# Output projection of a Hawk/HGRN2 step: low parts on VectorE, first touch of x2 on ScalarE with x1 added by DMA, the last head's small products over all four pairs

## The chip, the cores and the metric

The kernel runs on one core of one Trainium2 chip. The core has a matrix engine (TensorE, PE in the profile; its weight loads are listed apart as PEld), a vector engine (VectorE, DVE), a scalar engine (ScalarE, ACT), a general engine (GpSimd, POOL) and a sync engine (SyncE, SP) that here only issues DMA transfers. ScalarE and GpSimd can issue transfers too. Each engine works through its own list of instructions in order and waits on semaphores for the others. The metric is the device time of one execution in microseconds; the time of a kernel is the median of its runs.

## The reference

One inference step of a two-layer decoder trunk on 1024 prompt tokens and 8 x 4 sample tokens: 1056 token columns (TOK). Layer 0 is a recurrent block (RG-LRU), layer 1 a gated linear recurrence with 8 heads (HGRN2); then a final RMSNorm. What matters here is the end of layer 1:

```python
def _hgrn_layer(x, g_norm, w_in, lb, o_gain, w_out, S0):
    ...
    o = o * lax.rsqrt(jnp.mean(o * o, axis=-1, keepdims=True) + EPS) * o_gain.reshape(H_B, DV_B).astype(jnp.float32)
    y = (o.reshape(Bsz, T, INNER_B) * jax.nn.silu(gate)).astype(x.dtype)
    return x + y @ w_out, S_T.astype(x.dtype)
```

`x` at this point is called x1 in the kernel (the output of layer 0), and `x + y @ w_out` is x2. Both have 1024 features, that is 8 rows of 128 partitions by 1056 columns of float32.

## The kernel before, in words

**High and low parts.** A float32 product is made of three fast products (`mm3`, lines 243 to 245). Each operand is split into a high part, a copy rounded by ScalarE (`S.copy`), and a low part, the value minus its high part. `subtract` (line 330) writes the subtraction for either VectorE or GpSimd. `low` makes the low part in another way: ScalarE writes the negated high part and an accumulating DMA issued by GpSimd (line 317) adds the value.

**The planner.** `Flow` collects all operations of a layer with their engine, an estimated duration, and the keys that they read and write. `plan` runs them through a model of the engines and fixes each engine's order; the operations are then issued in that order. An operation with `both=True` on VectorE is taken to be lengthened while GpSimd is at work: in the model it ends only after GpSimd's current work, whatever that work is (`free["POOL"]`).

**Heads.** Layer 1 goes through heads 0 to 7. The recurrence of a head is cut into four bursts of small products, `burst1` to `burst4`. `burst1(h)` holds the first levels of head h and the transposed keys and values of head h - 1; `burst2(h)` two more levels and the states of head h - 1 (its last state updates are VectorE's L1257, which free a PSUM bank for the product of line 1250); `burst3(h)` the output products of head h - 1 and two levels of h; `burst4(h)` the gating of head h - 1, the last levels of h and a part of its values. `seven` makes the projections of a head with seven block products in place of eight (Strassen's scheme, Winograd's form); the digits of an order such as `"126b74b53"` are these seven block products, each `b` is a place where the next burst goes in.

**Output projection.** For heads 0 to 5 y is kept in DRAM in the sums that the scheme needs (`ysum`). `youts` loads 21 of them as tiles of 528 columns, into what becomes the low part; ScalarE makes the high part (line 1623) and the low part is a subtraction, seven of them on VectorE and fourteen on GpSimd (`YSUB`). `seven_out` then makes two of the eight rows of x2 at a time: four pairs, each in the order that `LAST` gives for it. For each pair it loads four blocks of w_out of 384 columns, GpSimd makes four combinations of them (line 1673, `combine`), and each of the seven blocks is split: the high part by ScalarE (line 1665), the low part by GpSimd, as `BYDVE` is empty. Each of the seven steps makes two products of 264 columns into one of four PSUM banks, and VectorE adds what is in the bank to x2 (line 1687, `add`): 14 additions a pair. Before that x2 was filled with x1 by a load on SP's queue, one per row. The bursts that are left of head 7 and its gating go in at the `b` of `LAST`: two in each of the first three pairs, none in the last. After the gating of heads 6 and 7, `splits` splits their y.

**The end.** What heads 6 and 7 add to x2 is made by ordinary products (lines from 1751; the addition is line 1831) in three column ranges, row by row, with the final norm behind them.

Of the kernel before, what the change touches and what calls it, by code (L numbers as in the profile page):

```python
# [24 lines left out]
NW, NXO, NRAW = 4, 3, 3  # L25
K1 = 6
NMM = 3
BYDVE = ()
HC = 1
FQ0, FQ, GV = "1267b4b35", "12b675b43", "126b74b53"  # L30
SPOTS, SPOTS0 = (6, 9, 0, 2), (2, 5, -1, -1)
LAST = "12b675b43", "126b74b53", "12b675b43", "1267543"
K2 = 8 - K1
RM, SM = 3, 6
OUT = ((0, 424), (424, 376), (800, 256))
# [16 lines left out]
class Flow:  # L52
# [49 lines left out]
    def plan(self, key, stop=None):  # L102

        n = len(self.ops)
        left = [len(o[3]) for o in self.ops]
        ready = [0.0] * n
        wait = {e: [] for e in self.ENGINES}
        free = dict.fromkeys(self.ENGINES, 0.0)
        dma = 0.0
        for i in range(n):  # L110
            if not left[i]:
                wait[self.ops[i][0]].append(i)
        starts, ends, took, order = [0.0] * n, [0.0] * n, [0.0] * n, []
        for _ in range(n):
            t0, e = min((max(free[e], min(ready[i] for i in q)), e) for e, q in wait.items() if q)
            q = wait[e]
            i = min((j for j in q if ready[j] <= t0), key=lambda j: (key[j], j))
            q.remove(i)
            order.append(i)
            _, us, _, _, _, kb, _, both = self.ops[i]  # L120
            if both and free["POOL"] > t0:
                us = max(us, free["POOL"] - t0 + us - 0.13)
            starts[i] = t0
            free[e] = end = t0 + us
            if kb:
                dma = max(dma, t0 + 2.6) + kb / 250.0
                end = dma - 2.15 - kb / 250.0
            ends[i] = max(free[e], dma if kb else 0.0)
            took[i] = us
            if i == stop:  # L130
                break
            for j in self.after[i]:
                ready[j] = max(ready[j], end + self.lag(i, j))
# [78 lines left out]
def tile_trunk(ctx: ExitStack, tc: tile.TileContext, xT, prm, hc, w0, wg, wo0, w1, wo1, s_in,  # L212
# [34 lines left out]
    def run(*gens):  # L247
        for g in gens:
            for _ in g:
                pass  # L250
# [47 lines left out]
    with ExitStack() as l0:  # L298
# [24 lines left out]
            fl.add("DVE", 0.13 + 0.0011 * n, emit, r, w, prio, both=both)  # L323

        def pool(n, emit, r, w, prio=5):
            fl.add("POOL", 0.1 + 0.00245 * n, emit, r, w, prio)

        def subtract(e, n, b, x, a, r, w, prio):

# [605 lines left out]
    with ExitStack() as l1:  # L935
# [49 lines left out]
        def eight(*name):  # L985
            return [(*name, i, x) for i in range(2) for x in range(4)]
# [367 lines left out]

        def burst1(h):
            s = next(side)
            run(together([*([levels01(h, *s)] if h < H else []), *([keys_(h - 1, *s), values(h - 1, (1,), *s)] if h else [])]))

        def burst2(h):
            s = next(side)  # L1360
# [5 lines left out]

        def burst4(h):
            s = next(hg)
            run(together([*([gated(h - 1, *s)] if h else []), *([levels3264(h, *s), values(h, (0,))] if h < H else [])]))
            if h:  # L1370
                summed_y(h - 1)

# [251 lines left out]
                subtract(YSUB[j], HT, lo, lo.bitcast(F32), hi, (hk, lk), (lk,), 2)  # L1624
                youtput[p].append((hi, lo, (hk, lk)))

        YSUB = V, G, G
        youtput = {p: [] for p in range(1, 8)}
        for p in map(int, GV.replace("b", "")):
            youts(p)  # L1630
# [1 line left out]
        def splits(k, cs, eng):  # L1632

            for c in cs:
# [6 lines left out]
        old = [GK, [("s", i) for i in range(6)], eight("A", 0), eight("A1"), eight("B"), eight("B2"), [("VT", i) for i in range(4)],  # L1641
               [("Gc", l) for l in (1, 2, 4, 8, 16, 32)]]

        def seven_out(m, order, at):

            nonlocal rawq
            bursts = iter(at)
            u = 384
# [36 lines left out]
            def add(i, a, z):  # L1685
                o, ok = x2[i][:, a:a + QT], ykeys(Y2 + i, a, QT)
                dve(QT, lambda: V.tensor_tensor(o, o, z[0], op=ALU.add), (z[1], *ok), ok, 0)

            for c in order:
                if not c.isdigit():  # L1690
                    next(bursts)()
                    continue
                p = int(c)
                if p == steps[-1]:
                    rawq = [(o, k) for o, k in freed]
                hi, lo, wk = parts[p]
                for x in range(2):
                    ps, pk = chains[p in (2, 3, 5)][x]
                    new = p in (1, 2, 5) or apart and p == 3
                    ops = [(a[:, x * QT:x * QT + QT], b[:, x * QT:x * QT + QT], k) for a, b, k in youtput[p]]  # L1700

                    def emit(ps=ps, ops=ops, hi=hi, lo=lo, new=new):
                        for j, (uh, ul, _) in enumerate(ops):
                            w = slice(128 * j, 128 * j + 128)
                            mm3(ps[:, :QT], (hi[:, w], lo[:, w]), uh, ul, new and j == 0, j == 2, True)

                    pe(1.09, emit, (*wk, *(k for o in ops for k in o[2])), (pk,))
                    z = ps[:, :QT], pk
                    first, second = x * QT, HT + x * QT
                    if p == 1:  # L1710
                        add(m, first, z)
                    elif p == 2:
                        add(m, first, z)
                    elif p == 6:
                        add(m, second, z)
                    elif p == 7:
                        add(m + 1, second, z)
                    elif p == 4:
                        add(m + 1, first, z)
                    else:  # L1720
                        if p == 5:
                            add(m + 1, second, z)
                        if p == 3 or apart:
                            add(m, second, z)
                n = steps.index(p) + NW
                if n < 7:
                    split(steps[n])

        def then(*fs):
            return lambda: [f() for f in fs]  # L1730

        ends_ = [lambda: burst3(H - 1), then(lambda: burst4(H - 1), lambda: splits(6, range(NCH), V)), lambda: burst1(H), lambda: burst2(H),
                 lambda: burst3(H), then(lambda: burst4(H), lambda: splits(7, range(NCH), V))]
        for i, order in enumerate(LAST):
            seven_out(2 * i, order, ends_[2 * i:2 * i + 2])
        side = cycle(banks8[NMM:4])
        raws = cycle([r for r in rawq if r[1][0] == "raw"])

# [181 lines left out]
```

## Time and profile before

| | us |
|---|---|
| median of 3 runs | 1079.52 (1077.19 to 1080.65) |
| the profiled execution | 1078.1 |
| its span, first to last instruction | 1076.3 |
| PE busy | 1045.6 (97%) |
| DVE busy | 788.9 (73%) |
| ACT busy | 667.1 (62%) |
| POOL busy | 543.9 (51%) |

A row of instructions names the line, the engine, the operation, and then output<-inputs by the program's tile names, with the count; a row of the timeline begins with its start and its duration in us, and in square brackets stand the idle time ahead of it and what ended that. A tile name is the name of the buffer: `xl` and `t` are operands of the output projection's `youts` as well as of the projections before it, `wlo` low parts of weights, `sg`, `ST`, `R`, `a` and `k` large buffers used for many things. The output projection's four pairs run from about 941 to 1035 us, the end from there to 1076.

### The profile page before, as it was taken

How to read it: one execution, taken by the hardware profiler on the slowest of the kernel's cores; microseconds unless marked ns; L12 is line 12 of the kernel's file. 1: busy time of each engine (PE TensorE's matmuls, PEld its weight loads, DVE VectorE, ACT ScalarE, POOL GpSimd, SP SyncE). 2: the span in 40 equal slices, each digit the busy share in tenths (PEclk: the TensorE clock that was granted, in tenths of full speed). 3: DMA queues.
4: the chain of work that ended last, by engine and by line, in shares of the span. 5: the costliest groups of instructions: out<-in, count | busy, mean ns of one | idle time of the engine just before them, and what ended most of it. 6: DMA issues, size and time to landing. Idle time of an engine off the chain costs nothing.

```text
span 1076.3 us, 25929 instructions
## 1 busy us (share of the span) xinstructions
PE 1045.6 (97%) x10092; PEld 1016.2 (94%) x10092; DVE 788.9 (73%) x1526; ACT 667.1 (62%) x1494; POOL 543.9 (51%) x566
## 2 busy tenths in 40 slices
PE   9999999999999999999979999999999999889996
PEld 9999999999999999999979999999899989889995
DVE  7999996887997787283987555666566766988546
ACT  6578657867665964243577676868485846663333
POOL 3425353353543546455444454544545454679565
PEclk9999999999999999999999999999999999989998
DMA  9211112124832786364684665657485632754114
GB/s 297 63 28 42 56 49 71 58 61 127 260 113 65 211 255 186 102 236 141 175 200 100 145 145 120 157 116 167 102 199 114 152 109 84 257 165 139 58 35 162
DMA packets 90331, 143.24 MB, mean 133 GB/s; under 512 B 11104, under 2 KB 55904, under 8 KB 90208
## 3 DMA queue, kind: packets, MB, share of 16 engines
q1 hardware_dynamic: 75808, 116.79, 34.3%
q0 software_dynamic: 12096, 22.03, 12.4%
q10 hardware_dynamic: 2304, 2.77, 0.8%
q8 instruction: 79, 1.29, 0.5%
q14 instruction: 44, 0.36, 0.1%
HBM read 81.60 MB, written 33.05 MB: 107 GB/s over the span
## 4 chain that ended last, share of the span: by engine, by line
PE 80%; DVE 13%; DMA 3%; issue 2%; ACT 1%; POOL 1%; POOLq 0%; ACTq 0%; SPq 0%; DVEq 0%
PE mm L243 22%; PE mm L244 22%; PE mm L245 22%; PE hg L1058 2%; PE hg L574 1%; DVE xl L330 1%; DVE R L1040 1%; DVE t L330 1%; PE hg L1275 1%; PE hg L1167 1%; PE hg L1221 1%; PE hg L243 1%; PE hg L244 1%; PE hg L245 1%; PE hg L1277 1%
## 5 line engine op out<-in xcount | busy, mean ns | idle before, releaser
L243 PE MATMUL mm<-xh,whi 128*128 128x352 f32 (+1 forms) x1147 | 355.2, 310 | 10.5 <-DVE sg L1537 4.1
L244 PE MATMUL mm<-xl,whi 128*128 128x352 f32 (+1 forms) x1147 | 349.3, 305 | 0.0
L245 PE MATMUL mm<-xh,wlo 128*128 128x352 f32 (+1 forms) x1147 | 349.1, 304 | 0.0
L243 PEld LDWEIGHTS mm<-xh,whi 128*128 128x128 f32 x1147 | 216.3, 189 | 11.8 <-DVE sg L1537 5.0
L244 PEld LDWEIGHTS mm<-xl,whi 128*128 128x128 f32 x1147 | 216.4, 189 | 4.1 <-issue 2.6
L245 PEld LDWEIGHTS mm<-xh,wlo 128*128 128x128 f32 x1147 | 216.3, 189 | 0.0
L330 POOL TENSOR_TENSOR wlo<-wraw,whi 128x512 fp32r<-128x512 f32 (+1 forms) x83 | 112.5, 1363 | 98.5 <-ACT whi L385 75.4
L243 PE MATMUL mm<-t,whi 128*128 128x264 f32 x408 | 119.3, 292 | 1.1 <-ACT k L1514 0.6
L245 PE MATMUL mm<-t,wlo 128*128 128x264 f32 x408 | 116.6, 286 | 2.1 <-DMA wlo<-wraw 2.1
L244 PE MATMUL mm<-t,whi 128*128 128x264 f32 x408 | 116.5, 286 | 0.0
L506 DVE SCALAR_TENSOR_TENSOR k<-xb,prm_sb,k 128x352 f32<-128x352 f32 (+2 forms) x144 | 90.2, 637 | 10.7 <-ACT k L503 6.0
L245 PEld LDWEIGHTS mm<-t,wlo 128*128 128x128 f32 x408 | 77.4, 190 | 2.5 <-DMA wlo<-wraw 2.5
L243 PEld LDWEIGHTS mm<-t,whi 128*128 128x128 f32 x408 | 77.7, 190 | 2.1 <-ACT k L1514 0.8
L244 PEld LDWEIGHTS mm<-t,whi 128*128 128x128 f32 x408 | 77.8, 191 | 0.1
L317 POOL DMA_DIRECT2D wlo<-wraw x51 | 44.6, 887 | 61.6 <-ACT wlo L316 35.4
L1537 DVE TENSOR_TENSOR k<-mm,k 128x264 f32<-128x264 f32 x72 | 30.5, 430 | 53.8 <-PE mm L245 50.5
L589 POOL TENSOR_TENSOR k<-X 128x352 f32<-128x352 f32 x36 | 44.9, 1256 | 47.7 <-DVE R L590 38.5
L243 PE MATMUL mm<-yh,whi 128*128 128x352 f32 x153 | 49.9, 326 | 0.0
L317 POOL DMA_DIRECT2D wlo<-R x30 | 28.5, 951 | 41.3 <-ACT wlo L316 34.9
L245 PE MATMUL mm<-yh,wlo 128*128 128x352 f32 x153 | 49.4, 323 | 0.0
L244 PE MATMUL mm<-yl,whi 128*128 128x352 f32 x153 | 49.4, 323 | 0.0
L385 ACT CAST whi<-wraw 128x512 fp32r<-128x512 f32 (+1 forms) x63 | 36.3, 591 | 20.1 <-DMA wraw<-in_w_dram 11.3
(413 smaller groups left out, 2722.4 us busy)
## 6 DMA issues: line engine op xcount, KB each, us to landing
wraw<-in_w_dram SPq DMA_DIRECT2D x88, 256.0 KB, 3.1
wlo<-wraw POOLq DMA_DIRECT2D x51, 256.0 KB, 4.1
wlo<-R POOLq DMA_DIRECT2D x30, 256.0 KB, 4.2
wraw<-in_wo_dram SPq DMA_DIRECT2D x37, 192.0 KB, 2.5
ysum<-sg SPq DMA_DIRECT2D x9, 528.0 KB, 4.4
si<-in_s_in_dram SPq DMA_DIRECT2D x8, 512.0 KB, 4.4
R<-in_w_dram SPq DMA_DIRECT2D x16, 256.0 KB, 3.8
out_ss_out_dram<-si SPq DMA_DIRECT2D x8, 512.0 KB, 2.7
```

The source lines that it names most:

```text
L243: T.matmul(out, wh, xh, start=first, stop=False, skip_group_check=chained)
L244: T.matmul(out, wh, xl, start=False, stop=False, skip_group_check=chained)
L245: T.matmul(out, wl, xh, start=False, stop=last, skip_group_check=chained)
L317: fl.add("POOL", 0.93, lambda: G.dma_start(dst.bitcast(F32), src, accum_op=ALU.add), (*r, *w), w, prio, n / 2)
L330: emit = lambda: e.tensor_tensor(b, x, a.bitcast(F32), op=ALU.subtract)
L385: act(m, lambda hi=hi, raw=raw, m=m: S.copy(hi[:, :m], raw[:, :m]), rk, (hk,), prio)
L506: dve(u, lambda src=src, dst=dst, sh=sh, k=k: V.scalar_tensor_tensor(dst, sh(src, k), pc("cw", 12 * k + m), dst, op0=ALU.mult, op1=ALU.add ...
L574: fl.add("PE", 0.62, lambda ps=ps, i=i, c=c: T.matmul(ps[:96, :CH], gs[:, i, :], ST[:96, chunk(c)], start=True, stop=True), (("gs",), *((" ...
L589: pool(CH, lambda x=x, a=a, b=b: G.tensor_tensor(x, a.bitcast(F32), b.bitcast(F32), op=ALU.add), (ak, bk), (xk,), 3)
L1040: dve(n // 2, lambda sv=sv, dv=dv, s=s, f=f: V.tensor_tensor(dv[:, :, s, :], sv[:, :, s, :], f, op=ALU.mult), (*sk, *gk), dk if i == o els ...
L1058: T.matmul(ps[32 * j:32 * j + 32, n * w:n * w + w], B[:, o:o + 32], q(slice(o, o + 32)), start=True, stop=True, tile_position=(0, 32 * j))
L1537: dve(QT, lambda: V.tensor_tensor(o[0], z[0], u[0], op=ALU.add), (z[1], u[1]), (o[1],), 0)
```

## The change

1. `YSUB` and `BYDVE`: all 21 low parts of the `youts` and all seven low parts of w_out's blocks in each pair are made by VectorE.
2. `put`: the first thing written to a part of x2 is a ScalarE copy from PSUM (steps 1, 6, 7 and 4 of each pair); the later ones stay VectorE additions. x1 is no longer loaded into x2 at the start of a pair: at its end, two accumulating DMAs issued by GpSimd add x1 to the finished rows.
3. `LAST` and `ends_`: the bursts are taken one after the other over all four pairs: pair 1 gets `burst3(7)` and the values' transposes of head 7, pair 2 `burst4(7)` with the split of head 6's y and `burst1(8)`, pair 3 `burst2(8)` and `burst3(8)`, pair 4 `burst4(8)` with the split of head 7's y. `values` leaves `burst4(7)` and `burst1(8)` for that.
4. The buffers of x2's rows are given out in another order, so that each is free by then.
5. The planner: only GpSimd's tensor operations that go through `pool` hold VectorE in the model, no longer its DMA issues and powers. This touches both layers.

```diff
-BYDVE = ()
+BYDVE, BYDMA = (1, 2, 3, 4, 5, 6, 7), ()
...
-LAST = "12b675b43", "126b74b53", "12b675b43", "1267543"
+LAST = "12b675b43", "12b67b453", "12b675b43", "1b267543"
...
-            if both and free["POOL"] > t0:
-                us = max(us, free["POOL"] - t0 + us - 0.13)
+            if both and e == "DVE" and held > t0:
+                us = max(us, held - t0 + us - 0.13)
             starts[i] = t0
             free[e] = end = t0 + us
+            if both and e == "POOL":
+                held = end
...
         def pool(n, emit, r, w, prio=5):
-            fl.add("POOL", 0.1 + 0.00245 * n, emit, r, w, prio)
+            fl.add("POOL", 0.1 + 0.00245 * n, emit, r, w, prio, both=True)
...
-            run(together([... *([keys_(h - 1, *s), values(h - 1, (1,), *s)] if h else [])]))
+            run(together([... *([keys_(h - 1, *s), values(h - 1, (1,) if h < H else (), *s)] if h else [])]))
...
-            run(together([... *([levels3264(h, *s), values(h, (0,))] if h < H else [])]))
+            run(together([... *([levels3264(h, *s)] if h < H else []), *([values(h, (0,))] if h < H - 1 else [])]))
...
-        YSUB = V, G, G
+        YSUB = V, V, V
...
-        x2 = [Gs, KR[:, :TOK], R[:, 2], R[:, 1], Bs, B2, VT, Gc]
+        x2 = [Gs, KR[:, :TOK], R[:, 2], VT, R[:, 1], Gc, Bs, B2]
...
-                dma(x2[i], x1d[i], (), ykeys(Y2 + i, 0, TOK), 3, 528)
...
-                subtract(V if p in BYDVE else G, u, lo, raw, hi, (rk, hk), (lk,), 2)
+                if p in BYDMA:
+                    low(u, lo, raw, (rk,), (lk,), 2)
+                else:
+                    subtract(V if p in BYDVE else G, u, lo, raw, hi, (rk, hk), (lk,), 2)
...
+            def put(i, a, z):
+                o, ok = x2[i][:, a:a + QT], ykeys(Y2 + i, a, QT)
+                act(QT, lambda: S.copy(o, z[0]), (z[1],), ok, 0)
...
                     if p == 1:
-                        add(m, first, z)
+                        put(m, first, z)
                     elif p == 2:
                         add(m, first, z)
                     elif p == 6:
-                        add(m, second, z)
+                        put(m, second, z)
                     elif p == 7:
-                        add(m + 1, second, z)
+                        put(m + 1, second, z)
                     elif p == 4:
-                        add(m + 1, first, z)
+                        put(m + 1, first, z)
...
+            for i in (m, m + 1):
+                ok = ykeys(Y2 + i, 0, TOK)
+                fl.add("POOL", 0.93, lambda i=i: G.dma_start(x2[i], x1d[i], accum_op=ALU.add), ok, ok, 3, 528)
...
-        ends_ = [lambda: burst3(H - 1), then(lambda: burst4(H - 1), lambda: splits(6, range(NCH), V)), lambda: burst1(H), lambda: burst2(H),
-                 lambda: burst3(H), then(lambda: burst4(H), lambda: splits(7, range(NCH), V))]
+        ends_ = iter([lambda: burst3(H - 1), lambda: run(values(H - 1, (0, 1))), then(lambda: burst4(H - 1), lambda: splits(6, range(NCH), V)), lambda: burst1(H), lambda: burst2(H),
+                      lambda: burst3(H), then(lambda: burst4(H), lambda: splits(7, range(NCH), V))])
```

More of the change, by code (lines that the diff above doesn't have):

```diff
@@ L108, in plan @@
         free = dict.fromkeys(self.ENGINES, 0.0)
-        dma = 0.0
+        dma = held = 0.0
         for i in range(n):
@@ L1356, in burst1 @@
             s = next(side)
-            run(together([*([levels01(h, *s)] if h < H else []), *([keys_(h - 1, *s), values(h - 1, (1,), *s)] if h else [])]))
+            run(together([*([levels01(h, *s)] if h < H else []), *([keys_(h - 1, *s), values(h - 1, (1,) if h < H else (), *s)] if h else [])]))
         def burst2(h):
@@ L1368, in burst4 @@
             s = next(hg)
-            run(together([*([gated(h - 1, *s)] if h else []), *([levels3264(h, *s), values(h, (0,))] if h < H else [])]))
+            run(together([*([gated(h - 1, *s)] if h else []), *([levels3264(h, *s)] if h < H else []), *([values(h, (0,))] if h < H - 1 else [])]))
             if h:
@@ L1638, in splits @@
                 subtract(eng, CH, b, x, a, (*xk, ("yh", k, c)), (("yl", k, c),), 1)
-        x2 = [Gs, KR[:, :TOK], R[:, 2], R[:, 1], Bs, B2, VT, Gc]
-        old = [GK, [("s", i) for i in range(6)], eight("A", 0), eight("A1"), eight("B"), eight("B2"), [("VT", i) for i in range(4)],
-               [("Gc", l) for l in (1, 2, 4, 8, 16, 32)]]
+        x2 = [Gs, KR[:, :TOK], R[:, 2], VT, R[:, 1], Gc, Bs, B2]
+        old = [GK, [("s", i) for i in range(6)], eight("A", 0), [("VT", i) for i in range(4)], eight("A1"),
+               [("Gc", l) for l in (1, 2, 4, 8, 16, 32)], eight("B"), eight("B2")]
         def seven_out(m, order, at):
             nonlocal rawq
-            bursts = iter(at)
-            u = 384
+            bursts, u = at, 384
             slot = {n: (t[:, :u], k) for n, (t, k) in zip(("11", "21", "22", "12", "s"), rawq)}
@@ L1727, in seven_out @@
                     split(steps[n])
+            for i in (m, m + 1):
+                ok = ykeys(Y2 + i, 0, TOK)
+                fl.add("POOL", 0.93, lambda i=i: G.dma_start(x2[i], x1d[i], accum_op=ALU.add), ok, ok, 3, 528)
         def then(*fs):
             return lambda: [f() for f in fs]
-        ends_ = [lambda: burst3(H - 1), then(lambda: burst4(H - 1), lambda: splits(6, range(NCH), V)), lambda: burst1(H), lambda: burst2(H),
-                 lambda: burst3(H), then(lambda: burst4(H), lambda: splits(7, range(NCH), V))]
+        ends_ = iter([lambda: burst3(H - 1), lambda: run(values(H - 1, (0, 1))), then(lambda: burst4(H - 1), lambda: splits(6, range(NCH), V)), lambda: burst1(H), lambda: burst2(H),
+                      lambda: burst3(H), then(lambda: burst4(H), lambda: splits(7, range(NCH), V))])
         for i, order in enumerate(LAST):
-            seven_out(2 * i, order, ends_[2 * i:2 * i + 2])
+            seven_out(2 * i, order, ends_)
         side = cycle(banks8[NMM:4])
```

## The prediction

> **What bounds the kernel now.** I read the page first: how much of the span TensorE (PE) works, and what the chain that ended last is made of.
>
> ```profile
> span 1076.3 us, 25929 instructions
> ...
> PE 80%; DVE 13%; DMA 3%; issue 2%; ACT 1%; POOL 1%; POOLq 0%; ACTq 0%; SPq 0%; DVEq 0%
> ```
>
> TensorE sets the time, but 13% of the chain is VectorE (DVE), so there is a stretch where it leads. The busy time by stretch (columns: length, then busy us and count for PE, PEld, DVE, ACT, POOL, then granted clock, DMA share, GB/s) shows where.
>
> ```profile
> 917.00:932.00 15.00, 15.00 (x183) 14.77 (x182) 14.77 (x25) 11.51 (x28) 7.43 (x6) 1.00 0.89 292
> 932.00:944.00 12.00, 7.23 (x186) 6.31 (x185) 11.73 (x10) 4.30 (x12) 9.00 (x7) 1.00 0.43 156
> 944.00:957.00 13.00, 11.98 (x100) 11.39 (x98) 12.79 (x22) 9.99 (x33) 11.41 (x10) 1.00 0.58 178
> 957.00:974.00 17.00, 13.97 (x247) 12.86 (x248) 14.43 (x29) 7.15 (x18) 14.42 (x12) 0.80 0.49 159
> ...
> 1000.00:1035.00 35.00, 35.00 (x286) 34.16 (x286) 17.41 (x43) 11.96 (x39) 23.22 (x26) 1.00 0.20 63
> ```
>
> From 917 to 957, VectorE is busy 39.3 of 40 us, and from 932 PE is not. This is the end of the last head's projections and the first pair of the output projection. From 1000 PE is full and VectorE half empty. PE's waits between 930 and 975 (us in total, times, longest):
>
> ```profile
> PE hg L1250 <- DVE si L1257: 3.0, 1, 3.0
> PE mm L243 <- ACT os L1245: 2.5, 1, 2.5
> PE mm L243 <- issue: 2.2, 1, 2.2
> ```
>
> That is 7.7 us. Two of the three lead back to VectorE: ScalarE's copy L1245 itself waited for VectorE's L1065, which stood behind three long instructions. Their rows, then POOL's of the same time:
>
> ```profile
> ACT os L1245 <- DVE attns L1065: 7.7, 1, 7.7
> ```
> ```profile
> 932.35 5.34 DVE L330 TENSOR_TENSOR xl<-xl,xh 128x528 fp32r<-128x528 f32 x1
> 937.62 2.51 DVE L1049 TENSOR_TENSOR sg<-sg 128x264 f32<-128x264 f32 x1
> 940.05 1.52 DVE L330 TENSOR_TENSOR t<-t,t 128x528 fp32r<-128x528 f32 x1
> ```
> ```profile
> 931.82 1.51 POOL L1199 TENSOR_TENSOR vb<-vst,bm 96x512 fp32r<-96x512 f32 x1
> 933.29 2.57 POOL L330 TENSOR_TENSOR xl<-xl,xh 128x528 fp32r<-128x528 f32 x2
> 935.83 1.29 POOL L330 TENSOR_TENSOR t<-t,t 128x528 fp32r<-128x528 f32 x1
> 937.10 1.45 POOL L330 TENSOR_TENSOR wlo<-wraw,whi 128x384 fp32r<-128x384 f32 x1
> ```
>
> With POOL idle, the same shapes take far less:
>
> ```profile
> 923.76 0.70 DVE L330 TENSOR_TENSOR xl<-xl,xh 128x528 fp32r<-128x528 f32 x1
> ...
> 942.51 0.68 DVE L1040 TENSOR_TENSOR sg<-sg 128x512 f32<-128x512 f32 x1
> ...
> 956.73 0.41 DVE L1687 TENSOR_TENSOR ST<-ST,mm 128x264 f32<-128x264 f32 x1
> ```
>
> So 9.37 us stand where 0.70 + 0.41 + 0.70 = 1.8 would do: 7.6 us held. The 5.34 us row ends at 937.69, about 0.6 after the POOL row of 935.83 ends: VectorE was passed over by four POOL instructions in a row. [...]
>
> The clock adds to it: after the 3.0 us wait it is down, and so it was at 883, after a shorter one.
>
> ```profile
> 882.46 0.39 PE L243 MATMUL mm<-xh,whi 128*128 128x264 f32 x1 [1.83 <-DVE sg L1537]
> ```
> ```profile
> 883.00:887.00 4.00, 4.00 (x22) 4.00 (x21) 2.99 (x9) 1.99 (x4) 1.28 (x1) 0.57 0.09 34
> ...
> 959.00:966.00 7.00, 7.00 (x154) 6.52 (x155) 4.43 (x14) 2.95 (x8) 5.92 (x7) 0.57 0.47 142
> ```
>
> At 0.57 for 7 us, 7 x 0.43 = 3.0 us are lost; at 883, 1.7 us. [...] Here 1.83 us brought it about and two waits of 4.7 us together did not, so I treat the drop as a chance.
>
> **The change, part by part.** All of it is priced in the stretch 917 to 974, where VectorE leads.
>
> *Subtractions leave POOL.* Grouped rows of that stretch, VectorE first, then POOL (busy us, mean ns, idle before):
>
> ```profile
> L330 DVE TENSOR_TENSOR xl<-xl,xh 128x528 fp32r<-128x528 f32 x4 | 9.6, 2404 | 0.0
> L1040 DVE TENSOR_TENSOR R<-R,sg 128x512 f32<-128x512 f32 x4 | 4.6, 1144 | 0.0
> L330 DVE TENSOR_TENSOR t<-t,t 128x528 fp32r<-128x528 f32 x3 | 3.7, 1242 | 0.2 <-ACT t L1623 0.2
> L1552 DVE SCALAR_TENSOR_TENSOR sg<-sg,k 128x264 f32<-128x264 f32 x4 | 3.6, 913 | 0.0
> L1340 DVE TENSOR_TENSOR sg<-sg 128x528 f32<-128x528 f32 x3 | 2.9, 953 | 0.0
> L1049 DVE TENSOR_TENSOR sg<-sg 128x264 f32<-128x264 f32 x1 | 2.5, 2506 | 0.0
> ```
> ```profile
> L330 POOL TENSOR_TENSOR xl<-xl,xh 128x528 fp32r<-128x528 f32 x8 | 11.8, 1482 | 7.5 <-DMA xl<-ysum 7.5
> L330 POOL TENSOR_TENSOR t<-t,t 128x528 fp32r<-128x528 f32 x6 | 8.0, 1338 | 3.8 <-ACT t L1623 3.8
> L330 POOL TENSOR_TENSOR wlo<-wraw,whi 128x384 fp32r<-128x384 f32 x5 | 6.6, 1316 | 0.0
> L330 POOL TENSOR_TENSOR wlo<-R,whi 128x384 fp32r<-128x384 f32 x3 | 3.7, 1234 | 0.0
> ```
>
> Against clean durations (0.70, 0.68, 0.70, 0.41, 0.70, 0.41) the six VectorE groups carry 6.8 + 1.9 + 1.6 + 2.0 + 0.8 + 2.1 = 15.2 us of hold. The four POOL groups, all of which go, are 30.1 of POOL's 7.43 + 9.00 + 11.41 + 14.42 = 42.3 us: 71%. In proportion 10.8 us of hold go. The bounds are 0 (the long rows have another cause) and 15.2. I take 10.8: the holds come from POOL instructions back to back, and it is the back-to-back ones that leave.
>
> *They arrive on VectorE.* 14 of 528 columns at 0.70 are 9.8; 8 of 384 lie between the 264 and the 512 row (0.41 to 0.68), at 0.55 in proportion: 4.4. Neighbouring rows overlap by some 0.07 (937.69 against 937.62), 22 x 0.07 = 1.5 less. So +12.7.
>
> *First touch by ScalarE.* Each pair loses 8 of its 14 VectorE additions: 8 x 0.41 = 3.3 in the first pair. They become ScalarE copies of the shape of this row:
>
> ```profile
> 898.97 0.38 ACT L1514 COPY k<-mm 128x264 f32<-128x264 f32 x1 [0.38 <-PE mm L245]
> ```
>
> 8 x 0.38 = 3.0 us on ScalarE, busy 21.4 of 42 us from 932 to 974: no cost while it has that room; without it PE would wait for the PSUM bank that the copy frees, up to 0.38 a copy. Net on VectorE: 12.7 - 3.3 - 10.8 = -1.4 us, within -5.8 to +9.4. So VectorE's work hardly shrinks; what changes is where its delay lies. The holds lie ahead of exactly the instructions PE waits for, and only the real durations then differ from what the planner orders by. A subtraction of 0.6 can be put behind L1065; a hold cannot be moved.
>
> *What PE's waits become.* At the first two (4.7 us), 7.6 us of hold shrink to some 1.0 (L1199 stays, 932.35 to 933.33), and up to five of the new subtractions (5 x 0.63 = 3.1) may fall ahead: 3.5 us sooner, so 1.2 of the 4.7 stay; bounds 0 and 4.7 gained. Next late there is L1245 behind its product. At the third (3.0) I take half, 1.5, as the low-priority L1257 still stands in a full queue; bounds 0 and 3.0. The clock's 3.0: half, 1.5, as a wait of 1.5 may or may not bring the drop; bounds 0 and 3.0.
>
> *Small products spread.* The first pair loses burst 4 of the last head (and keeps the two `values` transposes); pair 2 gets bursts 4 and 1, pair 3 bursts 2 and 3, pair 4 burst 4 and the split of the last y. No instruction is added. In 1000 to 1035 VectorE is at 17.41 of 35, which hides it; were that cover gone, the last split's chain would hold the final products. I take 0.
>
> *x1 by accumulating DMA.* Eight loads leave SP's queue, eight issues join POOL's. The issue and the landing of the nearest kind, and of the loads that go:
>
> ```profile
> L317 POOL DMA_DIRECT2D wlo<-wraw x51 | 44.6, 887 | 61.6 <-ACT wlo L316 35.4
> ```
> ```profile
> wlo<-wraw POOLq DMA_DIRECT2D x51, 256.0 KB, 4.1
> ...
> sg<-x SPq DMA_DIRECT2D x3, 528.0 KB, 4.7
> ```
>
> 8 x 0.89 = 7.1 us on POOL, against the 30.1 that left. Each issue waits for the pair's last VectorE addition, and POOL's combinations for the next pair stand behind it; they are needed only some steps later. Only the last pair is near the end, by these rows of before:
>
> ```profile
> 1035.40 0.43 DVE L1687 TENSOR_TENSOR sg<-sg,mm 128x264 f32<-128x264 f32 x1 [0.67 <-PE mm L245]
> ...
> 1043.49 0.60 DVE L1831 TENSOR_TENSOR sg<-mm,sg 128x424 f32<-128x424 f32 x1 [0.56 <-PE mm L245]
> ```
>
> The issue comes at 1035.8 and lands 4.1 (the row) to 8.5 us (in proportion to 528 KB) later, 1039.9 to 1044.3, the second 0.9 later. The seventh row's final addition needs it at 1043.5: 0 to 1.7 late. I take 0, as the row of completed x2 can go first.
>
> *The planner* no longer lets POOL's DMA issues and powers hold VectorE, in either layer. Orders shift everywhere; the size of one such wait elsewhere is the 1.83 above. 0, with two waits either way: +-3.
>
> **Sum.** 3.5 + 1.5 + 1.5 = 6.5 off. The profiled execution took 1078.1 (span 1076.3 and 1.8 around): 1071.6. The median of three runs, 1079.52, lies 1.4 above that execution, so 1073.
>
> **Rivals.** *Full relief*: the holds vanish and the planner places the new work behind what PE needs; all 7.7 + 3.0 go: 1079.5 - 10.7 = 1068.8. For: VectorE idles half of 1000 to 1035. Against: 12.7 us arrive.
>
> *A wash*: hold is exchanged for work one for one, and PE waits as before: 1079.5, give or take 3. For: the net of -1.4. This is also the case in which the change does not do what it says.
>
> *Slower, VectorE deeper in the lead*: it decides if less than 9.4 of the 15.2 us of hold go (12.7 - 3.3, 62%). If VectorE waited only for the one POOL instruction running, as the first 1.0 us of the 5.34, the rest having another cause, little hold would go: with 30%, 4.6, VectorE ends 4.8 later and PE waits that much more, with one more clock drop of 1.7: 1086. The end of the row just behind POOL's speaks against it. [...]
>
> *Slower by the planner or the tail*: one or two new waits or the late DMA, after the relief came to little: some 1083.
>
> **How the numbers follow.** Likeliest case 0.51 (its own range 1070 to 1076), full relief 0.15, wash 0.13, VectorE deeper in the lead 0.12, planner or tail 0.09. A difference under 0.3% (3.2 us) can hardly be told from no change. Faster 0.51 + 0.15 = 0.66, same 0.13, slower 0.21. The range leaves out the worst of the slower cases and the best of full relief: 1066.5 to 1081.5.
>
> **What would show it.** Right: VectorE's 528-column subtractions near 0.7 us throughout, the wait at L1245 under 1.5 us, no clock of 0.5 behind L1250, POOL's L330 gone from the output projection. Wrong: long VectorE rows without POOL beside them; PE waiting for `whi` or `wlo` of L330 in the pairs; a wait at the last products for the accumulating DMA or for the last head's split; new waits before 900.

## The result, and the profile after

The changed kernel takes 1075.72 us (median of 22 runs, 1072.80 to 1080.99) against 1078.63 for the kernel before on the same chip (22 runs): a ratio of 0.9973, 95% interval 0.9961 to 0.9986. So it is faster by 2.9 us, with an interval of 1.5 to 4.2: less than the 0.3% that the prediction gave as hardly to be told from no change, but with so many runs no change is excluded. The forecast was 6.5 us and 1073.0. The profiled execution took 1074.69 us. From its page: the span, the busy times, and the shares of the chain that ended last.

```profile
span 1072.9 us, 25911 instructions
...
PE 1046.7 (98%) x10092; PEld 1018.4 (95%) x10092; DVE 783.4 (73%) x1536; ACT 675.9 (63%) x1526; POOL 510.3 (48%) x532
...
PE 86%; DVE 8%; DMA 3%; ACT 1%; issue 1%; POOL 0%; ACTq 0%; POOLq 0%; DVEq 0%; SPq 0%
```

VectorE's share of the chain fell from 13% to 8%: the stretch in which it led has shrunk. Since both kernels make the same 6096 products in `mm3`, that stretch can be measured by counting them (the first has number 0): from the 5300th product (916.9 us before, 923.1 after) to the 5700th, and from there to the 6000th. The windows of the two kernels (columns as in the prediction), before first:

```profile
916.94:998.75 81.81, 72.73 (x921) 69.12 (x920) 73.43 (x129) 40.96 (x106) 62.76 (x53) 0.96 0.54 177
998.75:1044.44 45.69, 45.69 (x346) 44.64 (x345) 22.46 (x52) 16.09 (x47) 28.88 (x31) 1.00 0.17 53
```
```profile
923.07:992.54 69.47, 67.00 (x887) 64.61 (x886) 65.89 (x130) 45.12 (x120) 27.89 (x22) 1.00 0.52 161
992.54:1040.92 48.38, 48.38 (x379) 47.06 (x378) 26.39 (x60) 21.85 (x65) 25.97 (x29) 1.00 0.56 119
```

The first stretch is 12.3 us shorter, the second 2.7 longer (small products were moved into it): 9.6 us gained in the output projection. VectorE carries as many instructions in the first (130 for 129) in 7.5 us less, the clock is at 1.00 for 0.96, and POOL's busy time fell from 62.8 to 27.9. PE's waits of the kernel after, from 905 to 1035, are two:

```profile
PE hg L1060 <- ACT t L1625: 1.8, 1, 1.8
PE mm L245 <- DVE ST L1694: 0.6, 1, 0.6
```

(Up to about line 1660, lines of this kernel are two higher than before's. In the later kernels with one rule for each layer they are three higher; in low_alone and low_ordered they are those of before.) But the 5300th product came 6.1 us *later* than before. The loss lies at the very start: the 200th product came at 57.6 us instead of 50.5. PE's waits in the first 60 us, before and then after:

```profile
PE mm L243 <- DVE sg L534: 0.6, 1, 0.6
```
```profile
PE mm L245 <- DVE sg L536: 3.8, 1, 3.8
```

Line 536 of the kernel after is line 534 of the kernel before, in layer 0, which the change touches by the planner's rule alone. In the timeline of the kernel after, VectorE and then POOL (start, duration):

```profile
31.45 1.16 DVE L442 TENSOR_TENSOR R<-R,xo 128x352 f32<-128x352 f32 x2
...
32.72 1.26 DVE L750 TENSOR_SCALAR smalls<-smalls 128x12 f32<-128x12 f32 x1
33.90 2.01 DVE L442 TENSOR_TENSOR R<-R,xo 128x352 f32<-128x352 f32 x2
35.84 0.51 DVE L536 TENSOR_TENSOR sg<-mm,R 128x352 f32<-128x352 f32 x1
```
```profile
31.56 1.14 POOL L456 TENSOR_TENSOR nr<-nr,mhalf 128x3 f32<-128x3 f32 x1 [1.34 <-DVE nr L454]
32.66 1.29 POOL L332 TENSOR_TENSOR yl<-wraw,yh 128x512 fp32r<-128x512 f32 x1
33.89 1.64 POOL L554 TENSOR_TENSOR gl<-wraw,gh 128x512 fp32r<-128x512 f32 x1
```

The multiplication that PE waited for (L536) stood behind an operation on 12 columns (L750) and two additions of squares (L442), which POOL's two subtractions held: 1.26 and 2.01 us, where the same shapes take 0.17 (the kernel before, at 29.60, with POOL idle) and, for two, 1.16 (the row of 31.45). In the kernel before, two fewer additions of squares stood ahead of it, and it ran beside the first of the same POOL subtractions unhindered: 0.52 us, where the row of 35.84 has 0.51 with POOL idle. One of its inputs, `mm`, is in PSUM. Over the two traces, of 562 VectorE instructions that read `mm` or `hg`, both in PSUM, beside a POOL operation (powers and DMA issues aside), none lasted over 0.03 us longer than the median of its shape without POOL; of 703 others beside such an operation 310 lasted over 0.1 us longer. VectorE, then POOL:

```profile
31.09 0.52 DVE L534 TENSOR_TENSOR sg<-mm,R 128x352 f32<-128x352 f32 x1
```
```profile
31.23 1.30 POOL L330 TENSOR_TENSOR yl<-wraw,yh 128x512 fp32r<-128x512 f32 x1
```

And after the wait the clock was down, which cost 5.00 x 0.30 + 5.00 x 0.39 = 3.5 us; with the 3.2 by which the wait grew that is 6.7 of the 7.1:

```profile
35.00:40.00 5.00, 3.60 (x16) 3.60 (x17) 4.46 (x10) 2.34 (x5) 1.40 (x3) 0.70 0.69 196
40.00:45.00 5.00, 5.00 (x20) 4.50 (x19) 3.71 (x8) 1.94 (x4) 0.00 (x0) 0.61 0.10 36
```

So the account of the two profiled executions, by products: +7.1 by the 200th, 2.0 more by the 2900th (the rest of layer 0; its cause was not followed), which makes +9.1, then -3.0 from there to the 5300th (the heads), -9.6 in the output projection, 0 at the end: -3.5, against -3.4 between the two times.

### The profile page after: what moved, and what is told of

It is laid out like the page before. It is cut to its first block, busy times and chain, and to the rows that moved or that the text cites. A ratio compares the mean times of both kernels' runs of the same rounds, so it can differ in the third digit from the quotient of the medians.

```text
span 1072.9 us, 25911 instructions
## 1 busy us (share of the span) xinstructions
PE 1046.7 (98%) x10092; PEld 1018.4 (95%) x10092; DVE 783.4 (73%) x1536; ACT 675.9 (63%) x1526; POOL 510.3 (48%) x532
## 4 chain that ended last, share of the span: by engine, by line
PE 86%; DVE 8%; DMA 3%; ACT 1%; issue 1%; POOL 0%; ACTq 0%; POOLq 0%; DVEq 0%; SPq 0%
PE mm L245 24%; PE mm L247 23%; PE mm L246 23%; PE hg L1060 2%; PE hg L1277 1%; PE hg L576 1%; PE hg L1169 1%; PE hg L1279 1%; PE hg L1223 1%; PE hg L245 1%; PE hg L247 1%; PE hg L246 1%; DVE t L332 1%; DMA wraw<-in_w_dram 1%; DMA a<-xn 1%; DVE sg L1042 1%
## 5 line engine op out<-in xcount | busy, mean ns | idle before, releaser
L332 POOL TENSOR_TENSOR wlo<-wraw,whi 128x512 fp32r<-128x512 f32 (+1 forms) x66 | 94.8, 1444 | 88.1 <-ACT whi L387 71.2
```

The costliest lines, as they stand in the source:

```text
L332: emit = lambda: e.tensor_tensor(b, x, a.bitcast(F32), op=ALU.subtract)
```

## The experiments

None of the twelve kernels leaves out a part of the computation. Three columns are by counted products from the profiled execution, whose own time is given: how much later than before the 2900th product came, the change from there to the 5300th, and the length from the 5300th to the 6000th.

| kernel | median us | ratio, 95% interval | profiled | by 2900th | to 5300th | 5300th to 6000th |
|---|---|---|---|---|---|---|
| before | 1078.63 | 1 | 1078.10 | 0 | 0 | 127.5 |
| after | 1075.72 | 0.9973, 0.9961 to 0.9986 | 1074.69 | +9.1 | -3.0 | 117.9 |
| layer0_old_rule | 1066.50 | 0.9886, 0.9862 to 0.9910 | 1065.19 | +0.2 | -3.1 | 117.8 |
| rule_alone | 1084.04 | 1.0048, 1.0028 to 1.0068 | 1084.15 | +8.4 | -0.3 | 125.1 |
| seed2_new_rule | 1069.47 | 0.9921, 0.9897 to 0.9944 | 1067.49 | +2.9 | -3.5 | 117.8 |
| seed3_new_rule | 1074.07 | 0.9967, 0.9951 to 0.9984 | 1075.73 | +7.7 | -1.3 | 117.8 |
| seed2_old_rule | 1072.21 | 0.9942, 0.9918 to 0.9967 | 1070.87 | +4.3 | -2.2 | 118.0 |
| low_alone | 1077.91 | 0.9996, 0.9974 to 1.0017 | 1080.79 | +0.4 | +3.0 | 126.8 |
| low_and_rule1 | 1075.86 | 0.9969, 0.9954 to 0.9983 | 1074.98 | -0.2 | -2.1 | 126.7 |
| low_ordered | 1075.92 | 0.9986, 0.9965 to 1.0006 | 1075.91 | -0.1 | +0.3 | 125.3 |
| low_undone | 1072.19 | 0.9937, 0.9910 to 0.9964 | 1072.19 | -0.3 | -1.0 | 123.4 |
| x1_undone | 1076.24 | 0.9982, 0.9964 to 0.9999 | 1078.08 | +0.1 | +2.0 | 125.4 |
| spread_undone | 1072.82 | 0.9950, 0.9931 to 0.9968 | 1076.30 | 0 | +3.1 | 121.8 |
| best_ordered | 1072.85 | 0.9945, 0.9925 to 0.9966 | 1074.38 | +0.8 | +1.3 | 121.4 |

Each ratio is against runs of the kernel before on the same chip, so a small difference is read from ratios rather than from medians. The traces also show how far one execution can be read. Eight of the twelve kernels keep before's order of TensorE, VectorE and ScalarE in layer 0; they lie from -0.3 to +0.8 by the 2900th product. Five kernels (after, layer0_old_rule and the three with another starting number of the search, below) have one and the same order of VectorE, ScalarE and GpSimd in layer 1; they lie within 0.2 us of each other in the last column, but from -3.5 to -1.3 in the column ahead of it.

### Is layer 0's loss the planner's rule, and a thing apart?

`layer0_old_rule` is the changed kernel with the old rule in layer 0 alone (`self.until` is set in that layer only); `rule_alone` is the kernel before with the new rule.

```diff
-            if both and e == "DVE" and held > t0:
-                us = max(us, held - t0 + us - 0.13)
+            busy = free["POOL"] if self.until else held
+            if both and e == "DVE" and busy > t0:
+                us = max(us, busy - t0 + us - 0.13)
```

> The changed kernel with the planner's old rule in layer 0 alone, so that layer 0's order on every engine is the one of before, and layer 1 is the changed one. Theory A: the changed kernel lost some 6 us before the output projection, 7 of them in the first 50 us, to a worse order that the new rule gave layer 0, and gained some 12 in the projection. Then this kernel keeps the 12 and loses nothing: 8 to 11 us under the changed kernel's median 1075.7 less what the heads gained, that is 1066 to 1069, and PE's 500th product is at 101 to 103 us as before, not at 109. Theory B: the late start is not the order's doing (another cause in the execution, such as when transfers land): then this kernel is within 3 us of the changed one, 1073 to 1079.

Measured 1066.50: the loss by the 2900th product is gone (+0.2), and the output projection keeps its 117.8. The loss and the gain are two things, and without the loss the kernel gains 12.6 us, twice the forecast.

> The kernel before with the planner's new rule in both layers and nothing else. Theory A: the rule alone costs the 9 us of layer 0 and gives back some 3 in the heads, and the projection's waits stay: 5 to 9 us slower than before, 1084 to 1088. Theory B: no cost of the rule, 1076 to 1081.

Measured 1084.04, 0.5% slower than before: +8.4 by the 2900th product. The rule alone makes layer 0 as slow as in the kernel after. In the output projection it takes 2.4 us off, not 9.6.

### Is it the rule itself, or the draw of the planner's search?

In layer 0 the planner improves its order by a random search. These kernels differ in its starting number only; the last has the old rule in layer 0.

```diff
-        rng = Random(1)
+        rng = Random(2)
```

> The changed kernel with another seed in the planner's random search over the first 60 us of layer 0. Theory F: the 9 us of layer 0 come from the new rule itself, which leaves out that POOL's powers hold VectorE: PE's 500th product is at 107 to 110 us again, and the time within 2 us of 1075.7. Rival: it was a poor draw of the search: the 500th product comes elsewhere, by 3 us or more.

> The changed kernel with a third starting number for the planner's random search in layer 0. If the 7 us that layer 0 lost by its 500th product were mostly the luck of that search, this draw puts the 500th product anywhere from 0 to 7 us later than in the kernel before, and the time at 1068 to 1076 accordingly; and between the 200th and the 2900th product it loses some 2 us more, as all kernels with the new planner rule did. If the rule itself puts orders at a disadvantage at the start, it loses 6 to 8 us by the 500th product again, and seed 2 was the exception.

> layer0_old_rule with the second starting number for the search in layer 0, under the old planner rule there. If the drift of 2 us between the 200th and the 2900th product belongs to the new rule, there is none here (within 0.7 us). If it only belongs to other draws, it is here too, 1.5 to 2.5. The 500th product tells how far draws under the old rule lie apart: -1 to +7 us against the kernel before; time 1066 to 1074 accordingly.

The 500th product, against before: under the new rule +7.1 (number 1, the kernel after), +1.1 (number 2), +5.3 (number 3); under the old 0 (number 1) and +2.3 (number 2). From there to the 2900th: +2.0, +1.8, +2.4, and under the old rule 0 and +2.0. So my theory that a drift of 2 us belongs to the rule fell with the last kernel, which drifts too. What is shown: the kernel before had the quickest of five orders drawn, and the other four cost 3 to 9 us by the 2900th product. Whether orders under the new rule are worse on the average can't be told from three against two. That the new rule fits these rows better is no help here: the row of 31.45 above takes 0.58 for each addition beside POOL's power (31.56), against 0.57 with POOL idle (1.14 for two, at 30.20), so this power holds nothing, as the new rule has it and against what theory F took for granted. The five kernels with the changed output projection also line up: 0.2, 2.9, 4.3, 7.7 and 9.1 by the 2900th product, and 1066.50, 1069.47, 1072.21, 1074.07 and 1075.72 us (ratios 0.9886, 0.9921, 0.9942, 0.9967 and 0.9973).

### What do VectorE's low parts bring alone?

`low_alone` is the kernel before with the low parts on VectorE and nothing else.

```diff
-BYDVE = ()
+BYDVE = (1, 2, 3, 4, 5, 6, 7)
...
-        YSUB = V, G, G
+        YSUB = V, V, V
```

> The kernel before with the low parts of the output projection all on VectorE and nothing else. Theory A (POOL's instructions held VectorE in front of what PE waits for): the waits ahead of the first pair fall, 3 to 7 us faster than before, and the 528-column subtractions of VectorE stand near 0.7 us. Rival (VectorE was simply full, and the 9 to 11 us of new work there lengthen PE's waits): 3 to 8 us slower.

Measured: a wash, 0.9996, which neither side had expected. Its window between the 5300th and the 5700th product, to be set beside the first window of before:

```profile
920.31:1001.37 81.06, 71.67 (x920) 69.07 (x919) 73.17 (x156) 40.94 (x104) 25.04 (x22) 0.94 0.54 177
```

VectorE does 27 instructions more in the same busy time (73.2 for 73.4). At the prediction's 0.55 to 0.70 us each, some 17 us of work arrived and as much hold went. That is about the exchange one for one. (The 528-column subtractions are not all at 0.70: the row of 931.82 below has four in 5.06.) And PE's waits became one (930 to 975):

```profile
PE hg L1058 <- DVE sg L1040: 9.4, 1, 9.4
```

The second-level scaling of head 7 (L1040) stands behind the new subtractions in VectorE's order:

```profile
931.82 5.06 DVE L330 TENSOR_TENSOR xl<-xl,xh 128x528 fp32r<-128x528 f32 x4
...
939.17 3.35 DVE L330 TENSOR_TENSOR t<-t,t 128x528 fp32r<-128x528 f32 x4
942.44 0.69 DVE L1040 TENSOR_TENSOR R<-R,sg 128x528 f32<-128x528 f32 x1
943.06 1.93 DVE L330 TENSOR_TENSOR t<-t,t 128x528 fp32r<-128x528 f32 x3
944.91 0.69 DVE L1040 TENSOR_TENSOR sg<-a,sg 128x528 f32<-128x528 f32 x1
```

`low_and_rule1` adds the new planner rule in layer 1 only (`held` is set as in the change), to see whether the rule is what puts that scaling early.

```diff
-            if both and free["POOL"] > t0:
-                us = max(us, free["POOL"] - t0 + us - 0.13)
+            busy = free["POOL"] if self.until else held
+            if both and e == "DVE" and busy > t0:
+                us = max(us, busy - t0 + us - 0.13)
```

> The kernel before with the low parts on VectorE and the planner's new rule in layer 1 only. In the run with the low parts alone PE waited 9.4 us in the second burst because VectorE's L1040 stood behind four 528-column subtractions of xl, two of wlo and four of t. Theory E: the old rule put them there; with the new rule L1040 comes earlier, that wait falls under 3 us, and the time is 4 us or more under 1079, 1070 to 1075. Rival: the order stays as bad, as the rule is not its cause: 1076 to 1080.

It isn't: the wait is still 9.4 and the stretch 126.7. The kernel gained in the heads instead (-2.1 where low_alone has +3.0).

`low_ordered` sets the order by hand: nine subtractions of `low_alone` are made to depend on that scaling (`("two", s)`).

```diff
-                    (*sk, *gk), dk if i == o else dk[:4], 3, True)
+                    (*sk, *gk), [*(dk if i == o else dk[:4]), *([("two", s)] if h == H - 1 and level == 2 else [])], 3, True)
...
-                subtract(YSUB[j], HT, lo, lo.bitcast(F32), hi, (hk, lk), (lk,), 2)
+                subtract(YSUB[j], HT, lo, lo.bitcast(F32), hi, (hk, lk, *([] if p in (1, 2, 3, 5) else [("two", 0), ("two", 1)])), (lk,), 2)
```

> This is low_alone with one thing more: nine of the 21 subtractions for the y sums (those of block products 6, 7 and 4) may not start before the second-level scaling of head 7 (the 528-column additions R<-R,sg and sg<-a,sg that burst 2's product waits for). The same instructions run, only their order on VectorE differs. If the place of that scaling in VectorE's order is what cost low_alone its gain, the wait of 9.4 us at that product shrinks to 4 to 5 us, and the kernel comes out at 1072 to 1075. If VectorE simply has too much to do there, whatever the order, another of PE's waits between 930 and 975 takes the place of this one, and the time stays at 1076 to 1079.

The order became what was wanted, and the wait fell from 9.4 to 3.0; but another came:

```profile
PE hg L1250 <- DVE si L1257: 3.4, 1, 3.4
PE hg L1058 <- DVE sg L1040: 3.0, 1, 3.0
```

Of 6.4 us less waiting in one place, the output projection kept 1.5 (126.8 to 125.3), and the ratio still takes in 1. So order was only a small part of it. In low_alone the 5300th product was 3.4 us later than before, the 5400th, just behind the long wait, 12.9, and the 5700th only 2.6: while PE waited, VectorE went on with work that had to be done anyway, and PE caught up. As long as VectorE is full, a wait moved is not a wait saved. I take it from this that VectorE must have less to do there.

### What does each other part take away?

Each of these takes one part back out of `layer0_old_rule`. `low_undone` puts the low parts back on POOL (`BYDVE` empty, `YSUB` = V, G, G).

> As the first kernel of this group (old rule in layer 0), but with the low parts on POOL as before; the spread small products, the ScalarE copies and the x1 DMAs stay. Theory A: if the low parts carry most of the 12 us, this is 5 us or more slower than the first kernel, and the long VectorE rows beside POOL are back. Rival: the spread and the first touch carry it; then within 3 us of the first kernel.

`x1_undone` loads x1 at the start of a pair again, and VectorE adds every bank to it:

```diff
+                dma(x2[i], x1d[i], (), ykeys(Y2 + i, 0, TOK), 3, 528)
...
-                        put(m, first, z)
+                        add(m, first, z)
...
-            for i in (m, m + 1):
-                ok = ykeys(Y2 + i, 0, TOK)
-                fl.add("POOL", 0.93, lambda i=i: G.dma_start(x2[i], x1d[i], accum_op=ALU.add), ok, ok, 3, 528)
```

> The changed kernel with the old rule in layer 0, and with x1 loaded into x2 at the start of each pair and every part added by VectorE as before; low parts and spread as changed. The low parts alone gave nothing (1077.9 against 1079.1), undoing them cost 5.7 us (1072.2 against 1066.5): something must work together with them. Theory C: it is the first touch, which takes 8 VectorE additions of 0.41 a pair and the wait for x1's loads off VectorE's queue: then this is 4 us or more above 1066.5. Rival: it is the spread, and this stays within 2 us of 1066.5.

`spread_undone` has `LAST`, `ends_`, `values` and the buffers of x2 as before.

> The changed kernel with the old rule in layer 0, and with the last head's bursts back at their places of before (two in each of the first three pairs, none in the last), and x2's buffers as before; low parts, ScalarE copies and x1 DMAs as changed. Theory D: the spread takes VectorE work out of the full stretch: 3 us or more above 1066.5, with PE waits near 955 to 970. Rival: within 2 us.

Measured 1072.19, 1076.24 and 1072.82: by the ratios 0.5%, 1.0% and 0.6% more than `layer0_old_rule`, that is 5.5, 10.4 and 6.9 us, each give or take 3 to 4 by the intervals. Between the 5300th and the 6000th product, where the parts act, each costs 5.6, 7.6 and 4.0; the rest is in the heads, where the orders differ too and one order alone scatters by 2.2. The three together, with the new rule in layer 1, gain only 9.7, less than the sum of 17.2: so parts need each other. For the low parts that is shown directly, 0.7 alone (127.5 to 126.8) against 5.6 undone; the other two were not run alone. The single shares are rough, as every edit plans layer 1 anew, and an order alone is worth up to 3.6 us in this stretch (`best_ordered`, below). `x1_undone` takes back two things, ScalarE's copies and the x1 transfers, which no run separates. Here are the windows from the 5300th to the 5700th product: layer0_old_rule, low_undone, x1_undone, spread_undone.

```profile
913.99:983.40 69.41, 67.01 (x888) 64.61 (x887) 65.86 (x130) 45.10 (x120) 27.93 (x22) 1.00 0.53 161
```
```profile
915.57:989.24 73.67, 69.35 (x887) 66.81 (x886) 63.07 (x100) 45.53 (x120) 61.92 (x53) 0.95 0.50 149
```
```profile
919.00:995.99 76.99, 68.39 (x888) 66.27 (x887) 68.02 (x142) 40.53 (x104) 22.46 (x20) 0.93 0.55 180
```
```profile
919.98:996.25 76.27, 71.36 (x921) 68.77 (x920) 67.23 (x143) 45.88 (x122) 29.49 (x25) 0.96 0.49 148
```

The third number in brackets is VectorE's count. Without the low parts it has 30 instructions fewer and is busy only 2.8 us less. The first touch takes 12 off it here, the spread 13, which move to where VectorE is half empty; PE's count falls by 33 with the spread. With both, VectorE has the count of the kernel before.

How long POOL held VectorE can be added up row by row. For each operation and shape, take the median duration of the rows that have no POOL instruction beside them, over all traces; what a row lasts beyond that, where it is more than 0.1 us, is hold. Between the 5300th and the 5700th product it comes to 21.8 us before, 20.7 in low_undone, 8.9 in layer0_old_rule and 8.8 in the kernel after, and 7.2 in low_alone. Every such row has a POOL instruction beside it. So moving the low parts took 11.8 us of hold away, not all of it, and that nearly paid for the 30 instructions. In low_undone the long rows are back, as expected, and one was again passed over by several POOL instructions: it ends about 0.6 us after the last of these three.

```profile
930.58 4.05 DVE L1043 TENSOR_TENSOR sg<-a,sg 128x528 f32<-128x528 f32 x1
```
```profile
930.06 1.50 POOL L1202 TENSOR_TENSOR vb<-vst,bm 96x512 fp32r<-96x512 f32 x1
931.52 1.29 POOL L333 TENSOR_TENSOR xl<-xl,xh 128x528 fp32r<-128x528 f32 x1
932.77 1.29 POOL L333 TENSOR_TENSOR t<-t,t 128x528 fp32r<-128x528 f32 x1
```

In all three undone kernels PE waits longest at the same product, burst 2's, for the same scaling (930 to 975):

```profile
PE hg L1061 <- DVE sg L1043: 3.1, 1, 3.1
```
```profile
PE hg L1061 <- DVE sg L1043: 8.6, 1, 8.6
```
```profile
PE hg L1061 <- DVE sg L1043: 4.9, 1, 4.9
```

For `spread_undone` I had expected the wait elsewhere, at 955 to 970.

### Can the best kernel be ordered better?

`best_ordered` makes all 21 subtractions of `layer0_old_rule` depend on the scaling.

```diff
-                subtract(YSUB[j], HT, lo, lo.bitcast(F32), hi, (hk, lk), (lk,), 2)
+                subtract(YSUB[j], HT, lo, lo.bitcast(F32), hi, (hk, lk, ("two", 0), ("two", 1)), (lk,), 2)
```

> This is layer0_old_rule with the same dependency for all of these 21 subtractions, so that none of them can stand ahead of the second-level scaling of head 7. If the order there is still worth something, PE's wait at burst 2's product (1.75 us) falls below 1 and the kernel comes out at 1064 to 1066, faster than 1066.5. If the first products of the output projection need the early subtractions as much, they wait in its place: 1066.5 to 1070.

Both expectations missed: 1072.85, over 6 us slower than `layer0_old_rule`. The wait of 1.7 at burst 2's product, the first line here, went, and another took its place:

```profile
PE hg L1061 <- ACT t L1626: 1.7, 1, 1.7
```
```profile
PE mm L246 <- DVE attns L1068: 3.7, 1, 3.7
```
```profile
934.06 4.61 DVE L333 TENSOR_TENSOR xl<-xl,xh 128x528 fp32r<-128x528 f32 x6
938.60 2.79 DVE L333 TENSOR_TENSOR t<-t,t 128x528 fp32r<-128x528 f32 x3
```

Nine subtractions now run in one piece, and L1068 behind them came late: 3.6 us in the output projection. The heads lost more (-3.1 became +1.3): layer 1 is planned as a whole, and a dependency near its end changed its order from the 21st VectorE instruction on. How much of these 4.4 us is the order can't be told to better than the 2.2 by which one order scatters there.

## Why the prediction was right and wrong

The direction was right, and the time lies in the range, 2.7 us above the forecast. But the sum came near by two errors of opposite sign: the output projection gained more than I took, and a loss that I had priced at 0, give or take 3, came to 9.1.

*Where the time goes.* Right. VectorE led, the holds were real, and the long rows had no other cause that the traces show. Of 15.2 us of hold in six groups I let 10.8 go, 71%; row by row, between the 5300th and the 5700th product, it was 13.0 of 21.8, 60%. The six groups were not all of it: from 917 to 974 the same count gives 19.7. The rival that VectorE would end deeper in the lead is out, and with it the hold of one POOL instruction only, which the row of 4.05 contradicts like that of 5.34. The sign that was named came nearly true, two rows of 1.5 aside (kernel after, 923 to 992.5):

```profile
L332 DVE TENSOR_TENSOR xl<-xl,xh 128x528 fp32r<-128x528 f32 x12 | 8.9, 770 | 0.0
L332 DVE TENSOR_TENSOR t<-t,t 128x528 fp32r<-128x528 f32 x9 | 7.1, 822 | 0.0
```

*The low parts.* Without the first touch the terms are 12.7 - 10.8 = +1.9 on VectorE; low_alone measured -0.3 between the 5300th and the 5700th product, and the rival "a wash" is what the low parts alone give: 0.9996. In all three parts together VectorE's busy time fell by 7.5 us, more than the -1.4 of the sum and beyond its bound of -5.8.

*First touch, and the spread.* This is the step that failed inside the output projection: the spread was priced at 0 because the work is hidden where it arrives. It was not asked what leaving is worth. It leaves a stretch where VectorE is full, and undoing it costs 4.0 us there. The first touch was costed by the additions that go, 3.3 us on VectorE in the first pair; undone, together with the x1 transfers, it costs 7.6, with a wait of 8.6 and a clock of 0.93 in place of 1.00.

*PE's waits.* Forecast 6.5 us off in all, of 10.7; measured 9.6 net in the output projection. The waits of 7.7 us between 930 and 975 became 1.8, and the clock stayed at 1.00. The rival "full relief", 10.7, came nearest for this part. The wait that stays is not the one I named (L1245) but burst 2's product:

```profile
940.05 0.69 DVE L1042 TENSOR_TENSOR sg<-a,sg 128x528 f32<-128x528 f32 x1
```
```profile
940.88 0.75 PE L1060 MATMUL hg<-R,sg 128*32 128x32 f32 x64 [1.76 <-ACT t L1625]
```

The profile puts it down to ScalarE's copy for a `youts` tile. But the product reads `sg`, which VectorE's scaling finished at 940.74, just ahead of it, and in best_ordered, where the scaling comes sooner, the wait is gone: so it is likely the scaling.

*x1 by accumulating DMA.* Right at 0. Issue and landing (minimum, median, maximum) of the kernel after:

```profile
L1737 POOL DMA_DIRECT2D sg<-x x3: 886/900/920, 993.8 to 1030.5; - x3
...
DMA to landing us min/median/max: 5.9/6.7/10.2
```

The median of 6.7 us lies within the 4.1 to 8.5 that I estimated, the longest beyond. From the 6000th to the 6090th product nothing was lost (-3.5 and -3.4 against before).

*The planner.* This is the step that decided the size. I priced two waits of 1.83 either way. The mechanism, new waits from shifted orders, is shown in layer 0. In the heads the thirteen changed kernels scatter from -3.5 to +3.1, of which 2.2 us come with one and the same order. For layer 0 the size was wrong: one wait at its start, with the clock at 0.70 and 0.61 behind it, was 6.7 us of it, and 2.0 more came by the 2900th product. Such a wait before 900 was also named as a sign of being wrong. The rival that priced this case came to 1083 because it took the relief as small; the wait came, and the relief was large.

## What to carry to other kernels

Where one engine leads in a stretch, count what each part of a change puts into that stretch *and what it takes out*; work moved to where it is hidden is worth what it leaves behind, and parts that are a wash alone can gain together. An edit of a scheduler's model is an edit of every order that it makes: price it by how far the orders it draws lie apart (here 9 us for five orders), and measure it by itself. Count a fixed sequence of products through both traces: it shows at once where time is lost and where it is gained, and here an exception for layer 0, which brings back the order that the kernel before had drawn, turned 2.9 us into 12.6.

## What the runs showed of the hardware that was not expected

- The clock fell to 0.70 and 0.61 behind one wait of 3.8 us at the start of layer 0, and nearly doubled its price. Behind the remaining wait of 1.8 us in the output projection it stayed at 1.00 in the kernel after, though behind a wait of 1.83 it was at 0.57 in the kernel before, and behind those of 2.2 and 2.5 there at 1.00 (938.77 and 942.93). So the length of a wait alone doesn't say whether it drops.
- A VectorE instruction with a single input was held as well: 1.26 us for 12 columns (the row of 32.72 above), beside POOL's subtraction of 32.66 to 33.95; the kernel before took 0.17 for it with POOL idle (at 29.60). POOL's power of three columns (31.56) held nothing, and of 93 VectorE instructions in the traces of before and after that had a power beside them and, DMA issues aside, nothing else of POOL, none lasted over 0.02 us longer than the median of its shape without POOL.
- One hold can outlast several POOL instructions that follow one another: the row of 4.05 above stood through three, that of 5.34 in the prediction through four.
